# Holding VectorE's sums of weight blocks until the square sums at the front of each MLP are issued

## The chip, the cores and the metric

The kernel runs on one core of a Trainium2 chip. The metric is the device time of one execution in microseconds (us). Shorter is better. The engines that matter here are TensorE (PE in the profile, its weight loads PEld), VectorE (DVE), ScalarE (ACT), GpSimd (POOL, which here issues accumulating transfers) and SyncE (SP, which issues all plain loads of weights). Each engine works through its own queue in order: an instruction that waits holds up all that stand behind it on that engine.

## The reference, cut to what matters

The program is a two-layer encoder trunk on 256 tokens of width 1024: attention of one kind in layer 0, of another in layer 1, and after each a squared-ReLU MLP. The change is at the front of the two MLPs.

```python
def rms_norm(x, g):
    y = x * lax.rsqrt(jnp.mean(x * x, axis=-1, keepdims=True) + RMS_EPS)
    return y * g

def sq_relu_mlp(xn, w1, w2):                 # w1: 1024 x 4096, w2: 4096 x 1024
    return jnp.square(jax.nn.relu(xn @ w1)) @ w2

for layer in range(2):
    ...                                      # x = x + mixer(rms_norm(x, norm_mix[layer]))
    x = x + sq_relu_mlp(rms_norm(x, norm_mlp[layer]), mlp_w1[layer], mlp_w2[layer])
return rms_norm(x, norm_final)
```

## The kernel before

**Products.** A product of 32-bit numbers is made of three matmuls in a shorter type (`mm3`): each operand is cut into a high part and a low part, and high x high, low x high and high x low are summed. `split` makes the two parts: ScalarE casts the high one, VectorE subtracts it from the source for the low one. For the activations the parts are `xh` and `xl` (`prepare`, lines 237 and 238), for a block of weights `whi` and `wlo` (lines 197 and 198). A block of weights arrives in a tile `raw`, of which there are four; there are three pairs of `whi` and `wlo`.

**The MLP.** The hidden width is worked in 16 groups j: `up(j)` multiplies the tokens by a block of w1 (48 matmuls of 128x256, in three ranges of the eight token blocks for j = 0) and squares the ReLU, `down(j)` multiplies by a block of w2 and gathers in PSUM. The order on TensorE is up(0), up(1), up(2), down(0), up(3), down(1) and so on, and the loads of weights come in that order too.

**Sums of weight blocks.** For the first 14 groups of w2 the four 512-wide blocks are multiplied in seven products instead of eight, which takes sums of blocks. Two of them come with the data: SP loads one block twice into a tile `sum` (three of them), and then POOL issues a transfer that adds two other blocks to it in flight (lines 139 and 140). The others are made by VectorE in `more_sums`: `raw[:, 3] = sum[:, 1] + raw[:, 0]` (line 172), which needs the accumulated `sum`, and `every` (line 173). Later `sum` itself is split (`sumh` by ScalarE, `suml` by VectorE). `split_piece` calls `more_sums` when it begins to split such a block, and `weight()` asks for splits two blocks ahead, so the first call, for down(0), is recorded when up(2) takes its weights.

**The front of an MLP.** `hand_over` ends the attention half. For each of four pairs of token blocks VectorE adds the projection to `x` (line 300) and the pair's `xh` and `xl` are made, at a raised priority. Then come the squares of `x` for the norm, in `add_squares`: ScalarE squares (line 243), VectorE adds into `squares` (line 245) and folds at the end (line 247). The norm's factor itself is applied after the MLP, so TensorE needs the square sums only at `columns` (line 253), just ahead of down(0). up(0) multiplies token blocks 0 to 3 first, then 4 and 5, then 6 and 7.

**What sets the order.** A scheduler lays the recorded instructions out engine by engine, by priority and by when it thinks that they are ready; `hand_over` already uses `tc.issue_after(ins)`, under which instructions traced in the block stand behind `ins` on the same engine. It adds no semaphore wait of its own.

Of the kernel before, what the change touches and what calls it, by code (L numbers as in the profile page):

```python
# [22 lines left out]
ALU = mybir.AluOpType  # L23
# [6 lines left out]
T = 256  # L30
# [19 lines left out]
def trunk(ctx, tc, a, out):  # L50
    nc = tc.nc
# [8 lines left out]
    def scratch(shape, name):  # L60

        n = int(np.prod(shape))
        v = work.tile([P, 512], F32, tag="scratch", name=name, bufs=12)[:, :n]
        if len(shape) == 2:
            v = v.rearrange("p (a b) -> p a b", b=shape[1])
        return v

    def half_tile(pool, name, bufs, tag="half"):
        return pool.tile([P, KT, T], F32R, tag=tag, name=name, bufs=bufs)
# [57 lines left out]
    plan_mlp(1)  # L127

    parts = {}
    state = {"loaded": 0, "split": (0, 0), "used": 0, "pool": None}  # L130

    def load_weight(pieces=1, before=lambda i: None):
        j = state["loaded"]
# [16 lines left out]
    def cut(j, i, n):  # L150
        w = specs[j][1] // n
        return slice(i * w, (i + 1) * w)

    def split_piece(eng=None):
        j, i = state["split"]
        _, _, n, seven = specs[j]
        state["split"] = (j, i + 1) if i < n - (not seven) else (j + 1, 0)
        if i == 0:
            parts[j][1:3] = (wsp.tile([P, WCH], F32R, tag=v, name=v) for v in ("whi", "wlo"))
            if seven:  # L160
                more_sums(parts[j])
        if i == n:
            parts[j][1:3], (raw, hi, lo) = split_sums(parts[j])
            return split(hi, lo, raw)
        raw, hi, lo = (z[:, cut(j, i, n)] for z in parts[j][:3])
        return split(hi, lo, raw, eng)

    def more_sums(part):

        raw, sums = part[0].rearrange("p (b n) -> p b n", n=BLK), part[3]  # L170
        every = state["pool"].tile([P, BLK], F32, tag="every", name="every", bufs=2)
        nc.vector.tensor_tensor(raw[:, 3, :], sums[:, 1, :], raw[:, 0, :], op=ALU.add)
        nc.vector.tensor_tensor(every, raw[:, 3, :], raw[:, 1, :], op=ALU.add)
        part.append(every)

    def split_sums(part):
        _, hi, lo, sums, every = part
        more = [state["pool"].tile([P, 2, BLK], F32R, tag=v, name=v, bufs=2) for v in ("sumh", "suml")]
        blocks = lambda z, t: [z[:, b * BLK:(b + 1) * BLK] for b in range(4)] + [t[:, b, :] for b in range(2)]
        return [blocks(hi, more[0]) + [every], blocks(lo, more[1])], (sums, *more)  # L180

    def prefetch(loads, splits):
        while state["loaded"] < min(loads, len(specs)):
            load_weight()
        while state["split"] < (min(splits, len(specs)), 0):
            split_piece()
# [9 lines left out]
    def split(hi, lo, src, eng=None):  # L196
        a = nc.scalar.copy(hi, src).ins  # L197
        return a, (eng or nc.vector).tensor_tensor(lo, src, hi.bitcast(F32), op=ALU.subtract).ins  # L198
# [32 lines left out]
    def two(z):  # L231
        return z.rearrange("p (f n) -> p f n", f=2)

    def prepare(k, n, xT, ts=slice(0, T)):

        v, hi, lo, gk = x[:, k, ts], xT[0][:, k, ts], xT[1][:, k, ts], gains[:, n * KT + k:n * KT + k + 1]
        return (lambda: nc.scalar.activation(hi, v, AF.Copy, scale=gk).ins,
                lambda: nc.vector.scalar_tensor_tensor(lo, v, gk, hi.bitcast(F32), ALU.mult, ALU.subtract).ins)  # L238

    def add_squares(b, s):  # L240

        q = scratch([2, T], "q") if b else two(s)
        nc.scalar.activation(q, x[:, 2 * b:2 * b + 2, :], AF.Square)
        if b:
            nc.vector.tensor_tensor(two(s), two(s), q, op=ALU.add)
        if b == 3:
            nc.vector.tensor_tensor(s[:, 0:T], s[:, 0:T], s[:, T:2 * T], op=ALU.add)

    def columns(s):

# [34 lines left out]
    def sum_tile():  # L285
        return work.tile([P, 2 * T], F32, tag="squares", name="squares", bufs=1)
# [5 lines left out]
    def hand_over(accs, last, n):  # L292

        xT = half_tile(act, "xh", 2), half_tile(act, "xl", 2)
        s = sum_tile()
        for b in range(4):
            last[b]()
            v, acc = x[:, 2 * b:2 * b + 2, :], two(accs[b])
            with tc.high_priority(NORM_PRIO):
                nc.vector.tensor_tensor(v, acc, v, op=ALU.add)  # L300
                for f in zip(*(prepare(k, n, xT) for k in (2 * b, 2 * b + 1))):
                    done = [step() for step in f]

        with tc.issue_after(done[0]), tc.issue_after(done[1]):
            for b in range(4):
                add_squares(b, s)
        return xT, s

    def open_accs():
# [113 lines left out]
    def turn_over(m, last, inv, n):  # L423
# [7 lines left out]
        def turn(t, h, pt):  # L431
            with tc.high_priority(NORM_PRIO):
                for k in range(4):
                    nc.tensor.transpose(pt[:, k * P:(k + 1) * P], y[t, h][:, k * P:(k + 1) * P], ident)
                v = x[:, 4 * h:4 * h + 4, tok(t)]
                nc.vector.tensor_tensor(v, pt.rearrange("p (k n) -> p k n", k=4), v, op=ALU.add)
                for k in range(4 * h, 4 * h + 4):
                    done = [step() for step in prepare(k, n, xT, tok(t))]
            if (t, h) == (1, 0):
                with tc.issue_after(done[0]), tc.issue_after(done[1]):  # L440
                    for b in range(4):
                        add_squares(b, s)
# [104 lines left out]
    def even(ep):  # L547
# [85 lines left out]
        def weights(k):  # L633
            for _ in range(WPARTS // 2):
                done = split_piece()
            held[k // 2] = parts[k // 2][1:]
            return done
# [5 lines left out]
        with tc.manual_schedule(engines={ENG.PE, ENG.Activation, ENG.DVE}):  # L643
            for k in range(KT):
                for i in ((0,), (1,), (2,), (3,), (4, 5), (), (6, 7), ())[k]:
                    feature(i)
                if k == 5:
                    add_squares(0, s)
                    add_squares(1, s)
                weights(k)  # L650
                c_of(k)
                if k < 6:
                    v_of(k)
            add_squares(2, s)
            add_squares(3, s)
            split_piece()
            split_piece()
            v_of(6)
            r = rstd(s)
            c_squares(0)  # L660
            split_piece()
            ins = split_piece()
            c_squares(1)
            v_of(7)
            state["used"] = 4
            for j in held:
                del parts[j]
# [362 lines left out]
    def phase(name, fn, *args):  # L1030
        with tc.tile_pool(name=name, bufs=1, reuse_waits="tile") as pool:
            return fn(pool, *args)

    accs, last = phase("even", even)
    xT, s = hand_over(accs, last, 1)
    xT, s, late = turn_over(*phase("mlp0", mlp_between, xT, s), 2)
    accs, last = phase("odd", odd, xT, s, late)
    xT, s = hand_over(accs, last, 3)
    phase("mlp1", finish, xT, s)

# [93 lines left out]
```

## Time and profile before

| what | value |
|---|---|
| three timed runs | 753.8, 754.21, 755.93 us (median 754.21) |
| profiled execution: its own time | 752.51 us |
| its span, first to last instruction | 750.7 us |
| granted TensorE clock, mean | 0.994 |
| busy time PE / DVE / ACT | 734.1 / 583.5 / 542.8 us |

The profile is one execution; its times are us from the first instruction. A row of the timeline gives start, duration, engine, line, operation, output and inputs, the count of instructions merged into it, and in brackets how long the engine had idled just ahead of it and which instruction ended the wait. The start of the next row on an engine can lie a little ahead of the end of the one before, since instructions overlap by some 0.07 us. The first MLP begins on TensorE at 115.49 us and the second at 561.85 us of the span.

### The profile page before, as it was taken

Reading aid. Unit: us, or ns where it says so; the run is one execution under the profiler, and the core shown is the slowest. Engines: PE = TensorE matmul, PEld = TensorE weight load, DVE = VectorE, ACT = ScalarE, POOL = GpSimd, SP = SyncE. Lnnn points to the kernel's source line nnn. Section 1 sums busy time; section 2 is a strip of 40 time slices with the busy share of each in tenths; the row PEclk is TensorE's granted clock in tenths of the full one; section 3 lists DMA queues with packets and bytes.
Section 4 is the critical chain, followed back from the end, with each engine's and each line's share of the span. In section 5 each row is a group of like instructions: output and inputs, shape, how many; then the busy total and the mean of one; then the engine's idle time right before and its main releaser. Section 6 shows DMA issues by size and latency. Waiting matters only on the chain.

```text
span 750.7 us, 13847 instructions
## 1 busy us (share of the span) xinstructions
PE 734.1 (98%) x5414; PEld 677.3 (90%) x5414; DVE 583.5 (78%) x1062; ACT 542.8 (72%) x1027; POOL 38.9 (5%) x47
## 2 busy tenths in 40 slices
PE   9999998999999999999999999999997999999996
PEld 6988998988898888999999999999997988888885
DVE  6888858988788858877768777677766988778757
ACT  7778967757655666888988988889855757656752
POOL 0100001110111010000000000000010110010000
PEclk9999999999999999999999999999998999999999
DMA  8772348999999643633444444445668999999611
GB/s 314 277 265 107 113 140 213 302 282 268 272 274 280 191 146 146 237 144 131 180 173 141 165 145 155 155 141 169 224 209 185 264 271 266 263 273 261 195 60 56
DMA packets 37762, 151.12 MB, mean 201 GB/s; under 512 B 3776, under 2 KB 5312, under 8 KB 28608
## 3 DMA queue, kind: packets, MB, share of 16 engines
q1 hardware_dynamic: 29792, 135.28, 52.3%
q0 software_dynamic: 7616, 14.68, 11.5%
q8 instruction: 42, 0.69, 0.4%
q10 hardware_dynamic: 288, 0.28, 0.1%
q14 instruction: 24, 0.20, 0.1%
HBM read 149.18 MB, written 1.05 MB: 200 GB/s over the span
## 4 chain that ended last, share of the span: by engine, by line
PE 90%; DMA 4%; DVE 2%; ACT 2%; issue 1%; SPq 0%; POOL 0%; POOLq 0%; DVEq 0%
PE acc L201 15%; PE acc L202 15%; PE acc L203 15%; PE w L201 11%; PE w L202 11%; PE w L203 11%; DMA sum<-in_w 3%; PE acc L389 3%; PE w L210 1%; PE w L982 1%; PE w L964 1%; PE acc L997 1%; ACT whi L197 1%; PE w L798 1%; DVE wlo L198 1%
## 5 line engine op out<-in xcount | busy, mean ns | idle before, releaser
L198 DVE TENSOR_TENSOR wlo<-raw,whi 128x512 fp32r<-128x512 f32 (+3 forms) x360 | 297.3, 845 | 80.1 <-ACT whi L197 79.4
L197 ACT CAST whi<-raw 128x512 fp32r<-128x512 f32 (+3 forms) x360 | 253.4, 744 | 132.7 <-PE w L202 109.7
L201 PE MATMUL w<-xh,whi 128*128 128x256 f32 x528 | 160.3, 304 | 0.0
L202 PE MATMUL w<-xl,whi 128*128 128x256 f32 x528 | 150.3, 285 | 7.9 <-DVE xl L238 7.9
L203 PE MATMUL w<-xh,wlo 128*128 128x256 f32 x528 | 150.0, 284 | 0.0
L201 PE MATMUL acc<-xh,whi 128*128 128x256 f32 x432 | 125.2, 290 | 0.0
L202 PE MATMUL acc<-xl,whi 128*128 128x256 f32 x432 | 122.3, 283 | 0.0
L203 PE MATMUL acc<-xh,wlo 128*128 128x256 f32 x432 | 122.3, 283 | 0.0
L202 PEld LDWEIGHTS w<-xl,whi 128*128 128x128 f32 x528 | 102.0, 193 | 14.6 <-DVE xl L238 8.3
L201 PEld LDWEIGHTS w<-xh,whi 128*128 128x128 f32 x528 | 101.7, 193 | 6.3 <-issue 3.8
L203 PEld LDWEIGHTS w<-xh,wlo 128*128 128x128 f32 x528 | 102.0, 193 | 0.0
L201 PEld LDWEIGHTS acc<-xh,whi 128*128 128x128 f32 x432 | 82.6, 191 | 1.3 <-issue 0.3
L202 PEld LDWEIGHTS acc<-xl,whi 128*128 128x128 f32 x432 | 82.6, 191 | 0.0
L203 PEld LDWEIGHTS acc<-xh,wlo 128*128 128x128 f32 x432 | 82.6, 191 | 0.0
L140 POOL DMA_DIRECT2D sum<-in_w x28 | 30.7, 1095 | 531.5 <-PE acc L203 258.6
L201 PE MATMUL acc<-whi,xh 128*128 128x384 f32 (+2 forms) x160 | 55.5, 349 | 0.1
L202 PE MATMUL acc<-wlo,xh 128*128 128x384 f32 (+2 forms) x160 | 55.0, 344 | 0.4 <-DVE wlo L198 0.4
L203 PE MATMUL acc<-whi,xl 128*128 128x384 f32 (+2 forms) x160 | 54.7, 342 | 0.0
L201 PE MATMUL w<-whi,hh 128*128 128x512 f32 (+1 forms) x108 | 42.9, 398 | 0.0
L202 PE MATMUL w<-wlo,hh 128*128 128x512 f32 (+1 forms) x108 | 41.6, 385 | 0.0
L203 PE MATMUL w<-whi,hl 128*128 128x512 f32 (+1 forms) x108 | 41.3, 382 | 0.0
L931 DVE TENSOR_TENSOR r<-acc,cosT 128x512 f32<-128x512 f32 x24 | 16.6, 691 | 27.7 <-ACT sw L929 27.7
(225 smaller groups left out, 1422.8 us busy)
## 6 DMA issues: line engine op xcount, KB each, us to landing
raw<-in_w SPq DMA_DIRECT2D x36, 1024.0 KB, 6.2
raw<-in_w_oqk SPq DMA_DIRECT2D x24, 1024.0 KB, 4.9
raw<-in_w SPq DMA_DIRECT2D x28, 768.0 KB, 6.0
sum<-in_w SPq DMA_DIRECT2D x28, 512.0 KB, 7.9
sum<-in_w POOLq DMA_DIRECT2D x28, 512.0 KB, 9.3
raw<-in_w_ov SPq DMA_DIRECT2D x16, 768.0 KB, 4.3
raw<-in_w_oe SPq DMA_DIRECT2D x4, 1024.0 KB, 6.4
raw<-in_w_oo SPq DMA_DIRECT2D x4, 1024.0 KB, 4.8
```

The costliest lines, as they stand in the source:

```text
L140: nc.gpsimd.dma_start(sums, blocks[:, 0:3:2, :], accum_op=ALU.add)
L197: a = nc.scalar.copy(hi, src).ins
L198: return a, (eng or nc.vector).tensor_tensor(lo, src, hi.bitcast(F32), op=ALU.subtract).ins
L201: nc.tensor.matmul(o, sh, mh, start=first, stop=False)
L202: nc.tensor.matmul(o, sh, ml, start=False, stop=False)
L203: nc.tensor.matmul(o, sl, mh, start=False, stop=last)
L210: nc.tensor.matmul(o[j], y[pb, 0, ts], z[pb, 1, :], start=n == 0, stop=n == 2)
L389: nc.tensor.matmul(m[n], whole, wh[b], start=first, stop=end)
L798: nc.tensor.transpose(pt[:, b * P:(b + 1) * P], pp[:, b // 2, (b % 2) * P:(b % 2 + 1) * P], ident)
L931: nc.vector.tensor_tensor(r1, pq.rearrange("p (f n) -> p f n", f=2), cosT.unsqueeze(1).broadcast_to([P, 2, T]), op=ALU.mult)
L964: nc.tensor.matmul(ss[i, j][rows, T:T + P], d["q12"][:, j, i * P + 64 * c:i * P + 64 * c + 64], d["k12"][:, j, 2 * i + c, :], start=True, ...
L982: nc.tensor.transpose(pt[:, b * P:(b + 1) * P], pp[:, b * P:(b + 1) * P], ident)
```

## The change

The last instruction of the square sums (line 247 before) is kept in `state["parts_done"]` by `hand_over`, and `more_sums` is recorded under `tc.issue_after` of it. So VectorE's two sums of weight blocks stand behind the square sums on VectorE. Nothing is computed in another way, and no instruction is added or removed. In the changed kernel the line numbers are higher by two from line 161 on and by one from line 306 on (line 172 becomes 174, line 365 becomes 366).

```diff
             if seven:
-                more_sums(parts[j])
+
+                with tc.issue_after(state["parts_done"]):
+                    more_sums(parts[j])
...
         if b == 3:
-            nc.vector.tensor_tensor(s[:, 0:T], s[:, 0:T], s[:, T:2 * T], op=ALU.add)
+            return nc.vector.tensor_tensor(s[:, 0:T], s[:, 0:T], s[:, T:2 * T], op=ALU.add).ins
...
         with tc.issue_after(done[0]), tc.issue_after(done[1]):
-            for b in range(4):
-                add_squares(b, s)
+            state["parts_done"] = [add_squares(b, s) for b in range(4)][-1]
```

The square sums inside `turn_over`, ahead of the second attention, are called as before. The scheduler's layout changes on VectorE and ScalarE within the first three or four groups of each MLP; SP's and POOL's queues keep their order, TensorE's too but for a few matmuls that change places with a neighbour.

**VectorE, front of the first MLP.** In the names, `raw_1674` and `sum_1671` belong to down(0), `wlo_1747` to up(2), `xl_1578` is the low part of the tokens, `x4` being the four blocks of one half. Before:

```order
L300 TENSOR_TENSOR x_73<-acc_1174,x_73 128x512
L172 TENSOR_TENSOR raw_1674<-sum_1671,raw_1674 128x512
L198 TENSOR_TENSOR wlo_1747<-raw_1580,whi_1746 128x1024
L238 SCALAR_TENSOR_TENSOR xl_1578<-x_73,gains_85,xh_1577 128x256 x4
L245 TENSOR_TENSOR squares_1579<-squares_1579,q_1657 128x512
L198 TENSOR_TENSOR wlo_1747<-raw_1580,whi_1746 128x1024
L245 TENSOR_TENSOR squares_1579<-squares_1579,q_1660 128x512
L173 TENSOR_TENSOR every_1821<-raw_1674 128x512
L245 TENSOR_TENSOR squares_1579<-squares_1579,q_1663 128x512
L198 TENSOR_TENSOR suml_1829<-sum_1671,sumh_1828 128x1024
L247 TENSOR_TENSOR squares_1579<-squares_1579 128x256
```

After:

```order
L302 TENSOR_TENSOR x_73<-acc_1174,x_73 128x512
L200 TENSOR_TENSOR wlo_1747<-raw_1580,whi_1746 128x1024
L240 SCALAR_TENSOR_TENSOR xl_1578<-x_73,gains_85,xh_1577 128x256 x4
L247 TENSOR_TENSOR squares_1579<-squares_1579,q_1657 128x512
L247 TENSOR_TENSOR squares_1579<-squares_1579,q_1660 128x512
L200 TENSOR_TENSOR wlo_1747<-raw_1580,whi_1746 128x1024
L247 TENSOR_TENSOR squares_1579<-squares_1579,q_1663 128x512
L200 TENSOR_TENSOR wlo_1820<-raw_1674,whi_1819 128x1024
L249 TENSOR_TENSOR squares_1579<-squares_1579 128x256
L174 TENSOR_TENSOR raw_1674<-sum_1671,raw_1674 128x512
```

The sum for down(0) has left its place ahead of the second half of `xl` and stands behind the fold of the squares. One piece of up(2)'s split, `wlo_1747`, still stands ahead of `xl`.

**VectorE, first MLP, up to the third h of up(1)** (`h_1802`; its high part is what ScalarE casts next). `raw_1817` is down(1)'s block, `wlo_1820` down(0)'s, `wlo_1910` up(3)'s. Before:

```order
L375 TENSOR_TENSOR h_1732<-h_1732 128x128
L198 TENSOR_TENSOR wlo_1910<-raw_1744,whi_1909 128x1024
L198 TENSOR_TENSOR hl_1735<-h_1732,hh_1734 128x768
L172 TENSOR_TENSOR raw_1817<-sum_1814,raw_1817 128x512
L198 TENSOR_TENSOR wlo_1910<-raw_1744,whi_1909 128x1024
L373 TENSOR_TENSOR h_1802<-h_1802 128x256
L173 TENSOR_TENSOR every_1941<-raw_1817 128x512
L374 TENSOR_TENSOR h_1802<-h_1802 128x128
L255 TENSOR_SCALAR ms_1896<-w_1893 128x2
L375 TENSOR_TENSOR h_1802<-h_1802 128x128
```

After:

```order
L200 TENSOR_TENSOR suml_1829<-sum_1671,sumh_1828 128x1024
L376 TENSOR_TENSOR h_1732<-h_1732 128x128
L200 TENSOR_TENSOR wlo_1820<-raw_1674,whi_1819 128x1024
L200 TENSOR_TENSOR wlo_1910<-raw_1744,whi_1909 128x1024
L200 TENSOR_TENSOR hl_1735<-h_1732,hh_1734 128x768
L200 TENSOR_TENSOR wlo_1910<-raw_1744,whi_1909 128x1024
L374 TENSOR_TENSOR h_1802<-h_1802 128x256
L174 TENSOR_TENSOR raw_1817<-sum_1814,raw_1817 128x512
L375 TENSOR_TENSOR h_1802<-h_1802 128x128
L257 TENSOR_SCALAR ms_1896<-w_1893 128x2
L376 TENSOR_TENSOR h_1802<-h_1802 128x128
```

`suml_1829`, which stood ahead of all work on `h_1732`, and the second `wlo_1820` now stand just around its third step. `every_1941` has moved behind the steps on `h_1802`.

**VectorE, front of the second MLP.** `raw_7007`, `sum_7004` and `suml_7162` are down(0)'s, `wlo_7080` is up(2)'s. Before:

```order
L300 TENSOR_TENSOR x_73<-acc_6624,x_73 128x512
L172 TENSOR_TENSOR raw_7007<-sum_7004,raw_7007 128x512
L198 TENSOR_TENSOR wlo_7080<-raw_6912,whi_7079 128x1024
L238 SCALAR_TENSOR_TENSOR xl_6910<-x_73,gains_85,xh_6909 128x256 x4
L245 TENSOR_TENSOR squares_6911<-squares_6911,q_6989 128x512
L198 TENSOR_TENSOR wlo_7080<-raw_6912,whi_7079 128x1024
L245 TENSOR_TENSOR squares_6911<-squares_6911,q_6992 128x512
L173 TENSOR_TENSOR every_7154<-raw_7007 128x512
L245 TENSOR_TENSOR squares_6911<-squares_6911,q_6995 128x512
L198 TENSOR_TENSOR suml_7162<-sum_7004,sumh_7161 128x1024
L247 TENSOR_TENSOR squares_6911<-squares_6911 128x256
```

After:

```order
L302 TENSOR_TENSOR x_73<-acc_6624,x_73 128x512
L200 TENSOR_TENSOR wlo_7080<-raw_6912,whi_7079 128x1024
L240 SCALAR_TENSOR_TENSOR xl_6910<-x_73,gains_85,xh_6909 128x256 x4
L247 TENSOR_TENSOR squares_6911<-squares_6911,q_6989 128x512
L247 TENSOR_TENSOR squares_6911<-squares_6911,q_6992 128x512
L200 TENSOR_TENSOR wlo_7080<-raw_6912,whi_7079 128x1024
L247 TENSOR_TENSOR squares_6911<-squares_6911,q_6995 128x512
L200 TENSOR_TENSOR suml_7162<-sum_7004,sumh_7161 128x1024
L249 TENSOR_TENSOR squares_6911<-squares_6911 128x256
L174 TENSOR_TENSOR raw_7007<-sum_7004,raw_7007 128x512
```

The same move as in the first MLP; here `suml_7162`, which also needs the accumulated tile, stands ahead of the fold.

**ScalarE, second MLP, around the reading of up(2)'s product** (`relu_7213`). Before:

```order
L372 ACTIVATE whole_7139<-relu_7133 128x128
L197 CAST whi_7242<-raw_7077 128x1024
L367 ACTIVATE h_7135<-relu_7133 128x2x2x128
L197 CAST whi_7272<-raw_7150 128x1024
L197 CAST hh_7137<-h_7135 128x768
L365 ACTIVATE relu_7213<-w_7146 128x512
L197 CAST whi_7272<-raw_7150 128x1024
```

After:

```order
L199 CAST whi_7242<-raw_7077 128x1024
L373 ACTIVATE whole_7139<-relu_7133 128x128
L368 ACTIVATE h_7135<-relu_7133 128x2x2x128
L199 CAST whi_7272<-raw_7150 128x1024
L366 ACTIVATE relu_7213<-w_7146 128x512
L199 CAST hh_7137<-h_7135 128x768
L373 ACTIVATE whole_7219<-relu_7213 128x128
L199 CAST whi_7272<-raw_7150 128x1024
```

`relu_7213` has moved ahead of the cast `hh_7137`.

More of the change, by code (lines that the diff above doesn't have):

```diff
@@ L129, in trunk @@
     parts = {}
-    state = {"loaded": 0, "split": (0, 0), "used": 0, "pool": None}
+    state = {"loaded": 0, "split": (0, 0), "used": 0, "pool": None, "parts_done": None}
     def load_weight(pieces=1, before=lambda i: None):
```

## The prediction

> **What bounds the kernel now.** I read the page first, then the waits of TensorE, then the timeline of the two stretches in which it waited, and last what VectorE, ScalarE and the transfers did there. TensorE is the bound, and the group that waits longest is one of its low-part products:
>
> ```profile
> PE 734.1 (98%) x5414; PEld 677.3 (90%) x5414; DVE 583.5 (78%) x1062; ACT 542.8 (72%) x1027; POOL 38.9 (5%) x47
> ...
> L202 PE MATMUL w<-xl,whi 128*128 128x256 f32 x528 | 150.3, 285 | 7.9 <-DVE xl L238 7.9
> ```
>
> TensorE is busy 98% of the span, and 7.9 us of its idle time has one cause: a product with `xl` waits for VectorE to make `xl` (line 238). The timeline has both places, at the front of each MLP. TensorE in the first:
>
> ```profile
> 115.49 0.28 PE L201 MATMUL w<-xh,whi 128*128 128x256 f32 x1
> ...
> 119.21 0.28 PE L201 MATMUL w<-xh,whi 128*128 128x256 f32 x1
> 122.27 0.39 PE L202 MATMUL w<-xl,whi 128*128 128x256 f32 x1 [2.78 <-DVE xl L238]
> ...
> 135.84 0.50 PE L253 MATMUL w<-mean,squares 128*128 128x1 f32 x4
> ...
> 138.37 0.39 PE L201 MATMUL w<-whi,hh 128*128 128x512 f32 x1
> ```
>
> From 115.49 to 119.21 TensorE issues 32 matmuls, so one takes 3.72 / 31 = 0.12 us. Then it idles 2.78 us until `xl` of token block 4 is there. The columns of the square sums (line 253) start when up(0), up(1) and up(2), 3 x 48 = 144 matmuls, are done. They would take 144 x 0.12 = 17.28 us; they took 135.84 - 115.49 = 20.35 us. **The first front loses 3.07 us.** VectorE there:
>
> ```profile
> 115.57 1.28 DVE L300 TENSOR_TENSOR x<-acc,x 128x512 f32<-128x512 f32 x2
> 119.99 0.69 DVE L172 TENSOR_TENSOR raw<-sum,raw 128x512 f32<-128x512 f32 x1 [3.15 <-DMA sum<-in_w]
> 120.60 1.22 DVE L198 TENSOR_TENSOR wlo<-raw,whi 128x1024 fp32r<-128x1024 f32 x1
> 121.74 1.66 DVE L238 SCALAR_TENSOR_TENSOR xl<-x,gains,xh 128x256 fp32r<-128x256 f32 x4
> ```
>
> The sum of line 172 waited 3.15 us for the accumulated `sum` tile (its bracket). `wlo` of up(2) and the four `xl` need nothing of it, but VectorE works in order and they stood behind. The second front:
>
> ```profile
> 561.85 0.28 PE L201 MATMUL w<-xh,whi 128*128 128x256 f32 x1
> ...
> 570.87 0.58 PE L202 MATMUL w<-xl,whi 128*128 128x256 f32 x1 [5.14 <-DVE xl L238]
> ...
> 586.31 0.50 PE L253 MATMUL w<-mean,squares 128*128 128x1 f32 x4
> 568.60 0.69 DVE L172 TENSOR_TENSOR raw<-sum,raw 128x512 f32<-128x512 f32 x1 [5.27 <-DMA sum<-in_w]
> 565.73:570.87 5.14, 0.00 (x1) 0.00 (x0) 2.27 (x4) 2.49 (x3) 0.97 (x1) 0.74 1.13 206
> 570.87:575.05 4.18, 4.18 (x20) 4.18 (x21) 4.18 (x8) 1.05 (x1) 0.00 (x0) 0.51 0.49 85
> ```
>
> TensorE idles 5.14 us; line 172 waits 5.27 us. The windows (columns: PE, PEld, DVE, ACT, POOL busy, granted clock, DMA share, GB/s) show a second price: the granted clock is 0.51 for the 4.18 us after the wait. The 144 matmuls took 586.31 - 561.85 = 24.46 us against 17.28, so **the second front loses 7.18 us**: 5.14 idle, about 2.0 at half clock. Together 10.25 us of 750.7 is the most that this change can give back here.
>
> **The change, part by part.** It adds no instruction; it moves lines 172 and 173 for down(0) behind the fold of the squares, and the scheduler moves neighbours with them. SP's and POOL's orders stay, so every transfer is issued in the same sequence, only earlier or later as buffers come free.
>
> *Does `xl` come in time?* One `wlo` still stands ahead of it and needs its `whi` from ScalarE:
>
> ```profile
> 116.07 1.03 ACT L197 CAST whi<-raw 128x1024 fp32r<-128x1024 f32 x1
> 117.02 1.71 ACT L237 ACTIVATE xh<-x,gains 128x256 fp32r<-128x256 f32 x4
> 562.56 1.03 ACT L197 CAST whi<-raw 128x1024 fp32r<-128x1024 f32 x1
> 563.50 1.70 ACT L237 ACTIVATE xh<-x,gains 128x256 fp32r<-128x256 f32 x4
> ```
>
> First MLP: `whi` ends at 117.10, `wlo` runs 1.14 us (120.60 to 121.74 above), so `xl` begins near 118.3. In the trace TensorE starts 0.53 us after the first `xl` starts (121.74 to 122.27): 118.8, and it wants it at 119.33. Second MLP: `whi` ends at 563.59, `xl` begins near 564.8, TensorE could go on at 565.3; without the wait it would want it near 565.6. The other three `xl` follow every 0.4 us, while TensorE takes 0.36 us to the next block and then 0.72 us for each of the later ones. So both waits go, by margins of 0.5 and 0.3 us: -3.07 and -7.18.
>
> *What is late next?* VectorE has the same work to do before TensorE reaches down(0), and TensorE now comes 3.07 and 7.18 us sooner. Its fourth product of down(0) (the row at 138.37, and 588.84 below) writes the bank that held up(2), so it needs the ReLU of up(2) on ScalarE, which stands behind casts that need VectorE. The rows of the first MLP:
>
> ```profile
> 125.09 1.05 ACT L197 CAST sumh<-sum 128x1024 fp32r<-128x1024 f32 x1 [3.44 <-DMA sum<-in_w]
> 127.47 0.63 ACT L367 ACTIVATE h<-relu 128x512 f32<-128x512 f32 x1
> 128.34 0.42 DVE L373 TENSOR_TENSOR h<-h 128x256 f32<-128x256 f32 x1
> ...
> 136.45 0.28 DVE L375 TENSOR_TENSOR h<-h 128x128 f32<-128x128 f32 x1
> 136.88 0.83 ACT L197 CAST hh<-h 128x768 fp32r<-128x768 f32 x1
> 137.61 0.59 ACT L365 ACTIVATE relu<-w 128x512 f32<-128x512 f32 x1
> ```
>
> ScalarE still waits at the cast of `sumh` for down(1)'s accumulated tile, at 125.09. The ReLU and the cast that stood between it and the h of line 367 now stand ahead of that wait, so h starts when the cast at 125.09 ends, at 126.1 instead of 127.47, and VectorE can take it at 126.7. VectorE's work from there to the last h of up(1) was 128.34 to 136.73, 8.39 us without a break. The new order has the same amount in that stretch: a `wlo` (1.14) has gone ahead of it and a `suml` (1.14) come in; `every` of down(0) has replaced that of down(1). So it ends at 126.7 + 8.4 = 135.1. Then `hh` (0.73 to the next start) and the ReLU (0.59): 136.4 to 136.5. TensorE wants the bank at 138.37 - 3.07 = 135.30. **A new wait of 1.2 us (bounds 0.5 and 2.0, for 0.7 us in ScalarE's steps).** The first front gives 3.07 - 1.2 = 1.9 us.
>
> The second MLP:
>
> ```profile
> 570.98 1.05 ACT L197 CAST sumh<-sum 128x1024 fp32r<-128x1024 f32 x1 [1.28 <-DMA sum<-in_w]
> 575.72 0.60 ACT L365 ACTIVATE relu<-w 128x512 f32<-128x512 f32 x1 [3.69 <-PE w L203]
> ...
> 577.15 0.64 ACT L367 ACTIVATE h<-relu 128x512 f32<-128x512 f32 x1
> 577.82 0.43 DVE L373 TENSOR_TENSOR h<-h 128x256 f32<-128x256 f32 x1 [0.80 <-ACT h L367]
> ...
> 581.71 1.23 DVE L198 TENSOR_TENSOR wlo<-raw,whi 128x1024 fp32r<-128x1024 f32 x1 [0.80 <-ACT whi L197]
> 582.93 0.96 DVE L198 TENSOR_TENSOR hl<-h,hh 128x768 fp32r<-128x768 f32 x1
> 587.22 0.40 PE L203 MATMUL w<-whi,hl 128*128 128x512 f32 x1
> ...
> 588.84 0.39 PE L201 MATMUL w<-whi,hh 128*128 128x512 f32 x1
> ```
>
> ScalarE's cast at 570.98 waits for a tile that lands at the same time as before and ends at 572.0. In the trace ReLU, one cast and h follow in 575.72 to 577.79, 2.07 us; here they need not wait for TensorE: h at 574.1. VectorE from the first h (577.82) to the end of `hl` (583.89) took 6.07 us with a wait of 0.80; in the new order one sum more (0.68, line 173's like the 0.69 of line 172) stands between: 6.07 - 0.80 + 0.68 = 5.95, so `hl` ends at 580.0. TensorE's first product with `hl` would come at 587.22 - 7.18 = 580.04: just in time. The single h tile is free at 580.0; h (0.64), a cast (1.05) and the ReLU (0.60), which now stands ahead of `hh`, end near 582.2 with overlaps of 0.05 to 0.1, against 588.84 - 7.18 = 581.66. **A new wait of 0.5 us (0 to 1.5).** The second front gives 6.7 us.
>
> *The rest of both MLPs.* TensorE comes 2 and 7 us sooner to weights that come no faster by themselves.
>
> ```profile
> 136.20:250.00 113.80, 113.80 (x716) 100.52 (x716) 96.40 (x124) 74.94 (x100) 11.28 (x11) 1.00 0.95 273
> SPq L146 <- DVE wlo L198: 82.8, 20, 14.6
> 144.87 0.69 DVE L172 TENSOR_TENSOR raw<-sum,raw 128x512 f32<-128x512 f32 x1
> ```
>
> The middle of the first MLP has TensorE busy without a gap, the 16 DMA engines 95% busy and VectorE 96.4 of 113.8 us. That looks tight. But SP spent 82.8 us waiting for VectorE to free a `raw` before issuing loads, so the stream is paced by buffers, not by the engines' rate: and those buffers come free sooner too. The load behind `wlo` of up(2) could go at 122.3 instead of 125.2, and at 568.8 instead of 573.8. The sum for down(2) is made at 144.87; a pair of groups is 48 x 0.12 of up plus about 5 of down, 10.7 us, so its use is after two more of them past 135.84, near 157. That is a reserve of several us that is given up once and not per group. I cost this at nothing; if the cover is gone it costs up to the whole gain (a rival below).
>
> *Sum.* -3.07 + 1.2 - 7.18 + 0.5 = **-8.6 us** (from -10.25 with no new wait to -6.75 with both at their upper bounds). The profiled execution took 752.51 us, 1.81 around its span of 750.7, and lies 1.70 under the median of 754.21. So 743.9 for such an execution and **745.6 us** against the median.
>
> **The rivals.**
>
> *The accumulated tiles land later.* The loads that now go sooner (122.3, 568.8) run while down(1)'s accumulating transfer is still in flight (to about 125.05 and 570.95): 2.75 and 2.15 us of overlap. If that transfer got half the engines, it would land 1.4 and 1.1 us later; if it stood still, 2.75 and 2.15. Each moves the ScalarE cast and all behind it, so the gain is 8.6 - 2.5 = 6.1 to 8.6 - 4.9 = 3.7 us: 748 to 750.5.
>
> ```profile
> sum<-in_w POOLq DMA_DIRECT2D x1, 512.0 KB, 9.2
> sum<-in_w POOLq DMA_DIRECT2D x28, 512.0 KB, 9.3
> ```
>
> Against it: down(1)'s transfer of the first front, with little beside it at its end, took 9.2 us, and the median of all 28, most of them amid loads, is 9.3. The Trainium skill's page "DMA: Bandwidth & Descriptors", section "Queues, rings and completion order", speaks for it: each DMA engine takes packets in turn from the queues that have work, so a second queue halves the first. By that the sum would be the 6.1 above; the two medians disagree with it, unless what limits this kind of transfer is something else than its share of turns.
>
> *The stream of weights is the bound.* With DMA engines at 95% TensorE, being ahead, would run out of weights some groups later and give it all back: 754, no change. For it speaks the DMA share, against it SP's waits. It decides if loads in the middle stage are late by more than the reserve above.
>
> *Slower: the wait moves and grows.* The chain from the accumulated tile over ScalarE's cast, VectorE's queue and `hh` to the ReLU now decides when down(0) goes on. If it makes TensorE wait at each down(0) as it did in the second front (5.14 us, then half clock, 7.18 in all), the first front loses 7.18 - 3.07 = 4.1 us and the second breaks even: 758.3. For that the chain would have to be 4 us longer than I make it, and it turns to a loss only when the first front's new wait is over 3.07 us. Against it: VectorE's stretch has been counted operation by operation. The page "TensorE: Matmul & The Clock Gate" of the Trainium skill, section "What's actually happening", has a window of about 3.4 us for this: an idle one drops the clock to half, and a busy one restores it, by estimate 1.7 us lost. The two waits here (2.78 us with no drop, 5.14 us with 4.18 us at 0.51) agree with it.
>
> **How the numbers follow.** The forecast, both waits gone and one or two small new ones, has 0.76. The late tiles have 0.13, since they have a rule and an overlap for them but the medians against; the stream as the bound 0.06; the slower case 0.05. Faster by over 0.3% (2.3 us, about what a measurement of this kernel can tell from no change) is 0.76 + 0.13 = 0.89; within it 0.06; slower 0.05. The forecast's own bounds are 754.21 - 10.25 = 744.0 and 754.21 - 6.75 = 747.5. Medians of three scatter by some 0.8 us, which makes the low end 743.2; the high end takes in the halved share of the first rival, 749.0.
>
> **What the changed profile would show.** TensorE's waits for `xl` of line 238 (240 then) are gone or under 0.3 us, and the clock stays near 1.00 in the second front. VectorE has a short idle ahead of the first h of each MLP instead of 3.15 and 5.27 us ahead of the sum. TensorE's 144 matmuls take about 17.3 us in each front, and a wait of 0.5 to 1.5 us stands in down(0), released by the ReLU or `hl`. POOL's transfers land 9 to 10 us after issue. From down(1) on TensorE has no gap. I am wrong if the gap in down(0) is over 2 us, if the accumulated tiles land later than 125.5 (counted from the same start of up(0)), or if new waits for weights appear in the middle of the MLPs.

## The result and the profile after

The changed kernel takes **743.76 us** (median of four runs, 743.37 to 743.82) against 754.17 us of before on the same chip. The ratio is 0.9856 with a 95% interval of 0.9839 to 0.9873: 10.4 us faster. The profiled execution took 743.37 us with a span of 741.6 and a mean clock of 0.998; that of before had taken 752.51 us, so the two traces differ by 9.1 us. Why the medians differ by more than the traces is a question of its own, answered with the clock below.

The changed kernel's page, its lines of the engines and of the low-part product:

```profile
PE 731.8 (99%) x5414; PEld 675.2 (91%) x5414; DVE 582.7 (79%) x1062; ACT 543.3 (73%) x1027; POOL 38.9 (5%) x47
...
L204 PE MATMUL w<-xl,whi 128*128 128x256 f32 x528 | 149.3, 283 | 0.0
```

TensorE's longest waits (what it waited for, releaser, us in all, times, longest):

```profile
PE acc L86 <- DVE warm L81: 1.2, 1, 1.2
PE w L203 <- DVE ms L257: 1.0, 1, 1.0
PE acc L204 <- DVE wlo L200: 0.4, 2, 0.2
```

The 7.9 us for `xl` are gone. One wait is new: 1.0 us for `ms`, the mean square that VectorE makes out of the columns (line 257). TensorE's timeline in the two fronts, from the first matmul of up(0) over the columns into down(0):

```profile
115.11 0.28 PE L203 MATMUL w<-xh,whi 128*128 128x256 f32 x1
...
132.39 0.50 PE L255 MATMUL w<-mean,squares 128*128 128x1 f32 x4
...
134.92 0.39 PE L203 MATMUL w<-whi,hh 128*128 128x512 f32 x1
...
558.37 0.28 PE L203 MATMUL w<-xh,whi 128*128 128x256 f32 x1
...
575.83 0.50 PE L255 MATMUL w<-mean,squares 128*128 128x1 f32 x4
...
579.55 0.50 PE L203 MATMUL w<-whi,hh 128*128 128x512 f32 x1 [1.04 <-DVE ms L257]
```

The first front takes 132.39 - 115.11 = 17.28 us (20.35 before), the second 575.83 - 558.37 = 17.46 (24.46 before). The fourth product of down(0) is the row at 134.92 in the first MLP, with no wait, and the row at 579.55 in the second, with 1.04 us. The changed kernel's windows over both fronts and over the second down(0) (length, then PE, PEld, DVE, ACT, POOL busy, granted clock, DMA share, GB/s):

```profile
115.11:132.39 17.28, 17.28 (x146) 17.28 (x145) 15.17 (x24) 14.01 (x23) 2.19 (x2) 1.00 0.95 239
558.37:575.83 17.46, 17.46 (x147) 17.32 (x146) 14.67 (x23) 13.96 (x22) 2.17 (x2) 1.00 0.88 208
575.83:582.19 6.36, 5.32 (x27) 3.96 (x25) 6.36 (x12) 4.73 (x7) 0.00 (x0) 1.00 0.90 226
```

The same window of before:

```profile
586.31:591.34 5.03, 5.03 (x27) 4.04 (x25) 4.95 (x10) 4.95 (x8) 0.00 (x0) 1.00 0.98 294
```

TensorE is busy and at full clock through both fronts. The second down(0) lasts 6.36 us instead of 5.03: the 1.04 us wait and 0.29 us around it. The changed kernel's timeline of VectorE and ScalarE, first front and then second:

```profile
117.91 1.67 DVE L240 SCALAR_TENSOR_TENSOR xl<-x,gains,xh 128x256 fp32r<-128x256 f32 x4
...
124.10 0.69 DVE L174 TENSOR_TENSOR raw<-sum,raw 128x512 f32<-128x512 f32 x1
126.50 0.42 DVE L374 TENSOR_TENSOR h<-h 128x256 f32<-128x256 f32 x1 [1.71 <-ACT h L368]
...
134.40 0.16 DVE L257 TENSOR_SCALAR ms<-w 128x2 f32<-128x2 f32 x1
134.52 0.29 DVE L376 TENSOR_TENSOR h<-h 128x128 f32<-128x128 f32 x1
...
124.89 1.05 ACT L199 CAST sumh<-sum 128x1024 fp32r<-128x1024 f32 x1 [1.91 <-DMA sum<-in_w]
...
135.64 0.59 ACT L366 ACTIVATE relu<-w 128x512 f32<-128x512 f32 x1
...
561.28 1.67 DVE L240 SCALAR_TENSOR_TENSOR xl<-x,gains,xh 128x256 fp32r<-128x256 f32 x4
...
579.15 0.28 DVE L376 TENSOR_TENSOR h<-h 128x128 f32<-128x128 f32 x1
579.35 0.15 DVE L257 TENSOR_SCALAR ms<-w 128x2 f32<-128x2 f32 x1
...
567.60 1.06 ACT L199 CAST sumh<-sum 128x1024 fp32r<-128x1024 f32 x1 [1.28 <-DMA sum<-in_w]
...
577.86 0.59 ACT L366 ACTIVATE relu<-w 128x512 f32<-128x512 f32 x1
```

`xl` starts 3.8 us sooner in the first front (117.91 against 121.74; 0.4 of it is the earlier start of up(0)). The sum of line 174 has lost its wait: when it stands behind the squares, its tile has landed. The 9.1 us between the traces are made up so: 0.38 before the first front, 3.07 and 7.00 in the two fronts, less the 1.33 us in the second down(0): 9.12. The 0.38 are scatter: in after_again, the same kernel, up(0) begins at 115.82.

### The profile page after: what moved, and what is told of

Read it like the earlier page. It is cut to its first block, busy times and chain, and to the rows that moved or that the text cites. A ratio compares the mean times of both kernels' runs of the same rounds, so it can differ in the third digit from the quotient of the medians.

```text
span 741.6 us, 13847 instructions
## 1 busy us (share of the span) xinstructions
PE 731.8 (99%) x5414; PEld 675.2 (91%) x5414; DVE 582.7 (79%) x1062; ACT 543.3 (73%) x1027; POOL 38.9 (5%) x47
## 4 chain that ended last, share of the span: by engine, by line
PE 91%; DVE 3%; DMA 2%; ACT 2%; issue 1%; SPq 0%; POOL 0%; POOLq 0%; DVEq 0%
PE acc L203 16%; PE acc L204 15%; PE acc L205 15%; PE w L203 11%; PE w L204 11%; PE w L205 11%; PE acc L390 3%; PE w L212 1%; PE w L983 1%; DMA sum<-in_w 1%; PE w L799 1%; PE w L965 1%; PE acc L998 1%; DVE wlo L200 1%; PE w L813 1%
```

## The experiments

Each kernel ran beside before on the same chip. before's medians there were 754.0 to 754.5 us.

| kernel | median us | ratio to before, 95% |
|---|---|---|
| first_only | 749.2 | 0.9923 to 0.9962 |
| second_only | 749.66 | 0.9917 to 0.996 |
| no_sum_wait | 744.17 | 0.9851 to 0.9891 |
| behind_xl | 743.87 | 0.9838 to 0.9885 |
| after_again | 743.79 | 0.9842 to 0.9883 |
| early_ms, early_ms_again | 742.35, 742.21 | 0.9831 to 0.9867, 0.9822 to 0.9863 |
| delay_1k | 747.54 | 0.9887 to 0.9934 |
| delay_short | 748.87 | 0.9898 to 0.995 |
| delay_long | 755.45 | 1.0001 to 1.0034 |

### One MLP at a time: first_only and second_only

```diff
-                with tc.issue_after(state["parts_done"]):
+                with tc.issue_after(state["parts_done"]) if state["parts_done"] else ExitStack():
                     more_sums(parts[j])
...
-            state["parts_done"] = [add_squares(b, s) for b in range(4)][-1]
+            parts_done = [add_squares(b, s) for b in range(4)][-1]
+            state["parts_done"] = parts_done if n == 1 else None      # second_only: n == 3
```

> The sums are held behind the square sums in the first MLP alone; the second front is as before. Theory (the gain is the wait of TensorE for xl behind the sum that waits for its accumulated tile, front by front): the first front's 144 matmuls take 17.3 us instead of 20.35, the second front keeps a wait of about 5 us and half clock after it; 2.8 to 3.6 us faster than before, 750 to 751.5. Rival (the gain is spread, since earlier buffers let the loads run ahead in the whole MLP): 5 us or more, and less than 10 us left for the other front.

> The sums are held in the second MLP alone. Theory: the first front keeps its wait of about 2.8 us; the second takes 17.4 us instead of 24.5 and pays the wait of 1.0 us for ms in down(0), 1.3 with the slow restart; 5.5 to 7.5 us faster than before, 746.5 to 748.5. With the run of the first MLP alone the two gains add up to the whole 10 us within 1 us. Rival (the two are not independent, the first front's gain is lost or doubled by the second): the sum misses by over 2 us.

Measured: 4.9 us faster (2.9 to 5.8 by the interval) and 4.45 us faster (3.0 to 6.3). The sum, 9.4, comes within 1.1 us of the whole change (10.4), about as the theory has it. Both sizes came out beside what was expected, one above and one below. For second_only the traces of before and of the changed kernel give 7.00 - 1.33 = 5.7 us, which its interval holds. TensorE's wait in the trace of first_only:

```profile
567.98 0.58 PE L204 MATMUL w<-xl,whi 128*128 128x256 f32 x1 [5.21 <-DVE xl L240]
```

The first front of second_only on TensorE:

```profile
115.55 0.28 PE L203 MATMUL w<-xh,whi 128*128 128x256 f32 x1
...
122.48 0.58 PE L204 MATMUL w<-xl,whi 128*128 128x256 f32 x1 [2.93 <-DVE xl L240]
...
138.66 0.50 PE L255 MATMUL w<-mean,squares 128*128 128x1 f32 x4
```

The windows of second_only around that wait:

```profile
118.29:121.70 3.41, 1.26 (x11) 1.05 (x9) 1.50 (x2) 3.41 (x6) 0.00 (x0) 1.00 1.05 318
121.70:125.11 3.41, 2.63 (x12) 2.63 (x13) 3.41 (x7) 0.01 (x1) 0.00 (x0) 0.50 0.45 84
125.11:128.52 3.41, 3.41 (x18) 3.41 (x18) 3.41 (x6) 1.77 (x3) 1.09 (x1) 0.50 0.54 151
128.52:131.93 3.41, 3.41 (x30) 3.41 (x30) 2.15 (x5) 2.48 (x4) 0.00 (x0) 1.00 1.03 257
```

second_only left the first front as it was before, and there it waited 2.93 us instead of 2.78. But its front lasted 138.66 - 115.55 = 23.11 us instead of 20.35, because the clock dropped to 0.50 from 121.70 to 128.52. So the wait of the first front costs 3.07 us in one execution and 5.83 in another. The 2.8 us between them are also what the profiled execution of second_only lacks: it is 752.51 - 749.59 = 2.9 us faster than that of before, not 5.7.

In before, 10 of the 31 executions timed beside these kernels have a mean clock of 0.994 and take 752.0 to 753.8 us; the other 21 have 0.988 to 0.992 and take 753.4 to 756.4. The second kind takes 2.2 us more on average. The trace of before was one of the first kind, its median is of the second. That fits the 1.3 us between the difference of the medians (10.4) and that of the traces (9.1). It also fits the size of first_only: 3.07 us, and 2.2 more in two thirds of the executions, near 4.6. A mean clock does not say where in the program the clock was low; that it is the first front is seen in the trace of second_only alone. But first_only, whose first front has no such wait, has 0.994 to 0.996 in all of its four executions.

### The wait or the place: no_sum_wait and behind_xl

no_sum_wait goes back to before's place of the sum, but in the first call of each MLP the sum adds two raw blocks, which need no accumulated tile (so down(0) computes another number). Its sums are held only behind the last x add:

```diff
+                with tc.issue_after(state["x_last"]):
+                    more_sums(parts[j], state["sums"] in (1, 15))
...
-        nc.vector.tensor_tensor(raw[:, 3, :], sums[:, 1, :], raw[:, 0, :], op=ALU.add)
+        nc.vector.tensor_tensor(raw[:, 3, :], raw[:, 2, :] if first else sums[:, 1, :], raw[:, 0, :], op=ALU.add)
```

> VectorE keeps the order of before: the sum of line 172 stands ahead of wlo and xl. But for the first block of each MLP it adds two blocks of raw instead of a block of the accumulated tile, so it waits for nothing that lands late (that block's sum is another number; all else is computed as before). Theory (the wait is the cost, the place alone is not): one operation of 0.6 us ahead of xl eats the margins of 0.5 and 0.3 us, waits of 0.1 to 0.4 us for xl remain, and the time is 743 to 745.5. Rival (it is the new order that helps, the square sums being done first): 751 to 755, like before.

Measured: 744.17 us (743.94 to 744.25), within 0.5 us of the changed kernel. VectorE's rows in its first front, then TensorE's in down(0) of both MLPs:

```profile
116.58 0.68 DVE L174 TENSOR_TENSOR raw<-raw 128x512 f32<-128x512 f32 x1
...
118.32 1.67 DVE L240 SCALAR_TENSOR_TENSOR xl<-x,gains,xh 128x256 fp32r<-128x256 f32 x4
...
136.27 0.50 PE L203 MATMUL w<-whi,hh 128*128 128x512 f32 x1 [1.02 <-DVE ms L257]
...
580.46 0.51 PE L203 MATMUL w<-whi,hh 128*128 128x512 f32 x1 [0.54 <-DVE ms L257]
```

TensorE no longer waits for `xl` at all: the 0.68 us sum ahead of `xl` does no harm; its wait for the tile did. What is left over is again a wait for `ms`.

behind_xl holds the sums behind the last `xl` only, so that the square sums stand behind the sum's wait:

```diff
-            state["parts_done"] = [add_squares(b, s) for b in range(4)][-1]
+            for b in range(4):
+                add_squares(b, s)
+        state["parts_done"] = done[1]
```

> The changed kernel with the sums held behind the second half's last xl only, so that VectorE may issue them ahead of the square sums. Theory (only xl matters: the square sums are wanted at the columns, some 6 us after the accumulated tile lands): no wait for xl in either front, 743.4 to 744.5 us as the changed kernel. Rival (the square sums, then behind the wait for the accumulated tile, come too late for the columns): a wait of 1 us or more ahead of the columns in each front, 745.5 to 748 us.

Measured: 743.87 us (743.68 to 744.13), beside 743.79 of after_again on another chip: both points tried behind `xl` give the same time. VectorE waits for the tile again there, 1.55 us at the sum of the second front, and TensorE for nothing ahead of the columns (for 0.52 and 0.26 us behind them).

### The new wait: early_ms

```diff
-        inv = inverse_columns(s)
+        with tc.high_priority(NORM_PRIO):
+            inv = inverse_columns(s)
```

> As changed, and the columns of the square sums with ms and its reciprocal at a raised priority: TensorE does them ahead of up(2)'s products, VectorE does ms some 6 us earlier. Theory (the wait of 1.0 us in down(0) of the second MLP is for the bank that ms still reads, late because ms stands behind h and two sums on VectorE): the wait and its restart go, 1.3 us faster than the changed kernel: 742.0 to 743.0 against 743.8. Rival (ReLU of up(2) or hl is late there anyway by about as much): a wait of 0.5 to 1.2 us stays with another releaser, and the time stays at 743.3 to 744.

Measured: 742.35 us (741.92 to 743.01). Then, together with the changed kernel on another chip:

> The changed kernel again, to stand beside early_ms and before on one chip: 743.4 to 744.0 us, and before at 752 to 755, scattered by whether the first front's short wait takes the clock down in an execution.

> The kernel of early_ms again, beside the changed kernel on one chip. Theory (the wait of about 1.0 us for ms in the second MLP, and what stands behind it, is the whole difference): 742.0 to 743.0 us, 1.0 to 1.5 us under the changed kernel. Rival (the 1.4 us between them were a difference between chips): both within 0.3 us of each other.

Measured: 743.79 us (743.33 to 744.21) and 742.21 us (742.02 to 742.58). The gain of 1.6 us is real, and early_ms is the best kernel of this study. The second MLP of early_ms, its columns, its `ms` and the end of its down(0):

```profile
571.23 0.50 PE L255 MATMUL w<-mean,squares 128*128 128x1 f32 x4
...
574.24 0.15 DVE L257 TENSOR_SCALAR ms<-w 128x2 f32<-128x2 f32 x1
...
581.41 1.02 PE L390 MATMUL acc<-every,whole 128*128 128x512 f32 x2
```

The end of that down(0) in the changed kernel:

```profile
581.73 1.02 PE L390 MATMUL acc<-every,whole 128*128 128x512 f32 x2
```

The first matmul of up(0) is at 559.41 there and at 558.37 in the changed kernel. Counted from it, the columns now lie inside the front, `ms` comes after 14.83 us instead of 20.98, and no other wait has taken its place. To the last row it is 22.00 us instead of 23.36.

### What a wait of TensorE costs: delay_short, delay_long, delay_1k

These three add to early_ms one VectorE instruction of no use ahead of the second half's `xl`, in three lengths (7, 21, 4 times 256 elements). It sums up a constant tile `idler` into a column `sink`, both made once at the start:

```diff
-                nc.vector.tensor_tensor(v, acc, v, op=ALU.add)
-                for f in zip(*(prepare(k, n, xT) for k in (2 * b, 2 * b + 1))):
-                    done = [step() for step in f]
+                added = nc.vector.tensor_tensor(v, acc, v, op=ALU.add).ins
+                ahead = ExitStack()
+                for _ in range(1 if b == 2 else 0):
+                    with tc.issue_after(added):
+                        ahead.enter_context(tc.issue_after(nc.vector.tensor_reduce(out=sink, in_=idler.unsqueeze(1).broadcast_to([P, 7, 256]), op=ALU.add, axis=mybir.AxisListType.XY).ins))
+                with ahead:
+                    for f in zip(*(prepare(k, n, xT) for k in (2 * b, 2 * b + 1))):
+                        done = [step() for step in f]
```

> The kernel of early_ms, with one more VectorE instruction in each MLP: a sum over 7 x 256 elements of a constant tile, issued after the x add of the third block pair and ahead of the second half's xl. Nothing of the result is changed. By the traces' 1.07 us for 1024 elements the sum takes some 1.9 us, and the second half's xl stood about 0.5 us ahead of their need, so TensorE should wait 1.3 to 1.9 us in each front, released by xl or by a wlo behind it. Theory (a short wait costs itself, and no clock): 742.4 + 2 x 1.6 = 745.6 us (744.5 to 747), granted clock 1.00 in both fronts. Rival (every wait of TensorE also costs clock, half of the wait again or more): 747.5 to 750. Rival (the delay is hidden): 742 to 743.

> As delay_short, but the sum runs over 21 x 256 elements, some 5.6 us, so that TensorE should wait 5.0 to 5.6 us in each front. Theory (a wait of more than about 3 us costs itself and a stretch of half clock behind it, worth 2 to 2.9 us as in the traces of before and of second_only): 742.4 + 2 x 5.3 + 2 x 2.0 to 2.9 = 757 to 759 us, the granted clock near 0.5 for some 4 us behind each wait. Rival (the wait alone is the price, and the low clock in the other traces came from something else in them): 742.4 + 10.6 = 752.5 to 754 us with the clock at 1.00 behind the waits.

Measured: 748.87 us (747.44 to 750.5) and 755.45 us (752.93 to 757.42, ten executions). No theory met both. The short delay cost more than a wait alone and lies in the range of the rival with a price in clock; the long one cost less than two full drops, with executions spread over 4.5 us from clock 0.997 to 0.988. The traces have the reason. TensorE's waits in the two fronts of delay_long:

```profile
122.75 0.39 PE L207 MATMUL w<-xl,whi 128*128 128x256 f32 x1 [1.90 <-DVE xl L243]
...
127.25 0.50 PE L206 MATMUL w<-xh,whi 128*128 128x256 f32 x2 [2.69 <-ACT xh L242]
...
571.39 0.39 PE L207 MATMUL w<-xl,whi 128*128 128x256 f32 x1 [2.02 <-DVE xl L243]
...
575.18 0.80 PE L206 MATMUL w<-xh,whi 128*128 128x256 f32 x2 [1.80 <-ACT xh L242]
```

Windows of delay_long around them:

```profile
122.31:125.72 3.41, 1.81 (x13) 1.61 (x13) 2.51 (x4) 0.00 (x0) 0.13 (x1) 1.00 0.39 73
125.72:129.13 3.41, 1.88 (x15) 1.89 (x16) 1.90 (x4) 2.38 (x4) 0.95 (x1) 1.00 0.43 56
569.45:572.86 3.41, 1.47 (x12) 1.47 (x13) 3.41 (x5) 1.05 (x1) 0.00 (x0) 1.00 1.11 201
572.86:576.27 3.41, 1.61 (x8) 1.32 (x8) 1.72 (x4) 2.37 (x4) 0.00 (x0) 0.50 0.69 125
576.27:579.68 3.41, 3.41 (x18) 3.41 (x18) 2.11 (x3) 0.04 (x1) 0.00 (x0) 0.50 0.15 34
```

The two waits of the first front (1.90 and 2.69 us) left the clock alone, the two of the second, no longer in sum (2.02 and 1.80), took it down. In the fronts of every trace the low clock lasts 3.4 us or twice that, and the two drops of delay_short lie 440.3 us apart, 129 times 3.413. So the clock seems to be set at the ends of fixed stretches of 3.41 us, by how busy TensorE was in the one that ended. I laid these stretches out in each trace from its own low time. Of those around a wait, the ones in which TensorE was busy for 1.81 to 2.17 us kept the full clock, and the ones with 0.68 to 1.50 us were followed by the low one. One does not fit as it stands, in delay_short, whose wait there was only 1.32 us:

```profile
129.66 0.58 PE L258 MATMUL w<-mean,squares 128*128 128x1 f32 x4 [1.32 <-DVE squares L252]
127.49:130.90 3.41, 2.09 (x19) 1.92 (x18) 3.41 (x10) 2.43 (x5) 0.00 (x0) 1.00 0.82 149
130.90:134.32 3.42, 3.42 (x19) 3.42 (x18) 3.42 (x4) 3.29 (x5) 0.00 (x0) 0.50 0.64 143
```

The stretch has 2.09 us and was followed by the low clock too. It holds the four matmuls of the columns, one column each; without their 0.44 us it has 1.65, and the one kept stretch that holds them 1.73. That they do not count is a guess made to fit this case, and no run tests it. With it the line lies at about half a stretch. The last matmuls of the program agree: a stretch with 1.73 us (second_only) and one with 1.71 (early_ms_again) kept the clock, one with 0.96 (delay_1k) was followed by the low one. The Trainium skill's page "TensorE: Matmul & The Clock Gate", section "What's actually happening", has such a free-running window of 3413 ns; the length agrees with the 3.41 us here, but it says that an idle window takes the clock down, and here a half-idle one did. In before's second front too the stretch ahead of the drop, 564.73 to 568.14, was not idle: it has 1.00 us of work.

By the line at half a stretch, whether a 2.78 us wait drops the clock is a matter of where it falls. As an estimate, it leaves more than 1.7 us in one stretch at (2 x (2.78 - 1.7) + 3.41 - 2.78) / 3.41 = 82% of the places. Before had the lower mean clock in 21 of 31 executions. The first wait of before's trace was split over two stretches, 1.91 and 2.13 us busy. By the same line a wait under 1.7 us does not do it alone; the 1.32 us of delay_short, with the columns right behind, are the case against. The changed kernel has no wait longer than 1.2 us, and its eight executions all have a mean clock of 0.997 to 0.999.

> As delay_short, with the sum over 4 x 256 elements, some 1.15 us by delay_short's 2.01 us for 1792. Theory (the granted clock falls at the end of a stretch of about 3.4 us of which TensorE was without work for more than about 1.7 us, as the traces' waits lie on those stretches; a wait below that costs itself alone): most of the delay fits into the 0.5 us that xl has in hand and into the idle time of VectorE, waits of 0 to 0.8 us in each front, no drop, so 742.2 to 743.9 us in every execution, spread under 1 us, clock 0.997 or above. Rival (delay and time go in proportion): 742.2 + 6.6 x 4 / 7 = 746 us. Rival (a short wait too can take the clock down by chance): executions scattered over 2 us or more.

Measured: 747.54 us (745.93 to 749.26), and the theory's number was wrong. TensorE's waits in the fronts of delay_1k:

```profile
129.13 0.58 PE L258 MATMUL w<-mean,squares 128*128 128x1 f32 x4 [1.92 <-DVE squares L252]
...
575.49 0.58 PE L258 MATMUL w<-mean,squares 128*128 128x1 f32 x4 [1.28 <-DVE squares L252]
```

Windows of delay_1k around them:

```profile
127.10:130.52 3.42, 1.50 (x13) 1.42 (x13) 2.29 (x7) 1.99 (x4) 0.00 (x0) 0.99 0.87 149
130.52:133.93 3.41, 3.41 (x19) 3.41 (x18) 3.41 (x7) 3.41 (x7) 0.00 (x0) 0.51 0.67 151
574.25:577.66 3.41, 2.17 (x18) 2.20 (x19) 3.08 (x7) 1.98 (x4) 0.00 (x0) 1.00 0.34 136
```

The delay for `xl` was indeed hidden, but the fold of the squares (line 252) had moved behind an h, and early_ms's columns stand early on TensorE, so TensorE waited there. I had looked at `xl` alone. In this trace the clock kept to the rule: the 1.92 us wait left one stretch half idle and dropped it for one stretch, the 1.28 us wait did not. But the executions scattered over 3.3 us, as the last rival had it. Whether waits like the 1.92 us or shorter ones made that scatter is not shown: one execution was traced, and delay_short has a 1.32 us wait with a drop behind it. All this was read off traces in hand; no run placed a wait at a chosen point of a stretch, so the half-stretch rule is fitted to seven stretches with a drop and six without, not proved.

## Why the prediction was right, point by point

The forecast was 745.6 us, the time 743.76: within the range, on the side foretold, by the mechanism foretold. Of the 1.8 us between them 0.5 is the sum (8.6, against 9.1 between the traces, 0.38 of them scatter ahead of the first front). The other 1.3 is the 1.70 us by which before's profiled execution lay under its median: the forecast carried it over, and in the changed kernel it was 0.39.

- **Both waits for `xl` go.** Right: -3.07 us in the first front as counted, -7.00 in the second against -7.18. no_sum_wait shows that the wait for the accumulated tile was the cause and not the 0.7 us of the sum itself. The second part of the second front, the half clock, went too.
- **Margins of `xl`.** `xl` was foretold for 118.3 and came at 117.91, with up(0) 0.38 us sooner. No wait was left.
- **The new wait of 1.2 us in the first front.** This step failed. It had the fourth product of down(0) write the bank of up(2), so that it would wait for the ReLU. The ReLU came where I put it (135.64 + 0.59, foretold 136.4), but the product ran at 134.92, before it. What it needs is the bank of the columns, which `ms` frees: the wait in the second MLP names it, and early_ms, which only moves the columns and `ms` forward, takes it away. In the first MLP `ms` ended at 134.56 and the product went at 134.92: mis-sized by 1.2 us, it was 0. The rows of before could not tell the two apart, since the product at 138.37 came behind both `ms` and the ReLU.
- **The new wait of 0.5 us in the second front.** Same step, other sign: 1.33 us, since `ms` stood behind the three steps on h and came at 579.35. Together the two new waits came to 1.3 us where 1.7 were foretold, so the wrong bank hardly shows in the sum. It would have sent anyone who wanted the last 1.5 us to ScalarE's ReLU instead of to `ms`.
- **The clock behind the first wait.** Costed at nothing, since the trace of before showed none. By the mean clocks it is there in two thirds of the executions, and in none of the eight of the changed kernel: as far as the runs show, this is the term missing from the forecast against the median. The prediction also took the two waits of before to agree with an idle window; the wait of 5.14 us does not, since the clock fell behind a stretch with 1.00 us of work.
- **The accumulated tiles land later.** Refuted. From the start of up(0) to the cast of `sumh` it was 125.09 - 115.49 = 9.60 us and is 9.78; 9.13 and 9.23 in the second front. In the changed kernel SP issued the loads at 122.14 and 565.51, while down(1)'s transfers were in flight, and from issue to landing the transfers took 9.2 and 10.6 us (9.2 and 10.3 before). By estimate, the taking of turns of the Trainium skill's page "DMA: Bandwidth & Descriptors", section "Queues, rings and completion order", would have made it 1.4 and 1.1 us later; 0.1 to 0.2 were seen. The median landing of all of POOL's transfers rose from 9.3 to 9.6.
- **The stream of weights as the bound.** Refuted: TensorE's list of waits has none in the middle of the MLPs, and the lead gained in the fronts was there at the end: the traces' ends differ by as much as the fronts.

## What to carry to other kernels

On an engine that works in order, look at what stands behind a wait, not at how long the waiting instruction takes: an add of 0.7 us, recorded early because its weights were wanted next, held up the activations for 3 to 5 us. Move such a wait behind what the bound engine needs first, and then ask which small instruction frees its next buffer, from the rows that name the releaser rather than from a count of banks. And where a mean clock differs between executions of one kernel, its short waits have a second price that a single trace may not show.

## What the runs showed of the hardware

- A wait of TensorE of about 2 to 3 us may or may not halve its clock: 2.78 us (before) and 2.69 us (delay_long) did not, 2.93 us (second_only) did, and so did 1.92 us (delay_1k). In delay_short the clock fell behind a wait of 1.32 us with the columns right behind the wait. The low clock lasted 3.41 us or 6.82 us; in second_only the 6.82 us cost 2.8 us on top of the wait.
- 1024 KB loads that started while an accumulating transfer of 512 KB was in flight left it at 9.2 us from issue to landing in the first front, and took it from 10.3 to 10.6 in the second.
